# hT, the low weight parts and oT at other places in SBUF

## The chip, the cores and the metric

The kernel runs on 1 core of one Trainium2 chip. The metric is the device time of one execution in microseconds. The time before is the median of three runs, 1087.04 us (1086.99 to 1087.83).

## The reference

One decoder layer on a residual stream of 256 positions and 2048 channels, in float32. Cut to what matters here:

```python
h = rmsnorm(x, pre_mix_g)
proj = h @ w_in                               # 2048 x 4368
q_a, k_a, v_a, q_b, k_b, v_b, f_b = split(proj)
o_a = swa_sink_attention(q_a, k_a, v_a, sinks)     # 16 heads of 64, window 128, ALiBi, sinks
o_b = forgetting_attention(q_b, k_b, v_b, log_sigmoid(f_b + b_forget))   # 16 heads of 64
x = x + rmsnorm(concat(rmsnorm(o_a), rmsnorm(o_b)) @ w_out, post_mix_g)  # 2048 x 2048
h = rmsnorm(x, pre_ffn_g)
u = causal_dwconv(h @ w_up, conv_w, conv_b)        # 2048 x 11264, width 3
gate, val = split(u)
x = x + rmsnorm((gelu(gate) * val) @ w_down, post_ffn_g)   # 5632 x 2048
```

## The kernel before

Every matrix product is made exact enough by splitting both float32 operands into a high part (rounded to float32r) and a low part (the rest), and by adding three products: high by high, high by low, low by high. All weights come from HBM once, in units of 128 partitions by up to 1024 floats, issued by SP into the tile raw (5 buffers). ScalarE copies a unit into its high part whi (L111), and VectorE subtracts to get the low part wlo (L114); each has 5 buffers. TensorE then uses them in one of two ways.

*hT moves, weights stay.* hT holds the transposed input of the projection, for each of 16 k-tiles 512 columns: 256 of the high part, then 256 of the low part. It is a tile of 128 x 16 x 512 floats. `proj_T` makes the product for 256 output channels: its `high(u)` (L256) takes 128 x 128 pieces of whi as the stationary operand and moves all 512 columns of hT; its `low(u)` (L263) takes pieces of wlo and moves only the 256 high columns. Four units of four k-tiles make one projection, in runs of several units, so that up to 32 matmuls of one kind follow each other. `unit_T` (L220 and L225) does the same in the first projections, `first_gate` (L878 and L874) in the first one of the MLP, half a k-tile's columns at a time. The up-projection (w_up) runs like this in two stretches, from 356.79 to 588.11 us and from 707.81 to 955.53 us.

*Weights move, activations stay.* `mm3` (L278) takes a 128 x 128 piece of an activation as stationary operand and moves whi, wlo and whi again past it. It is used with hT for v (384 or 272 columns), with oT for the output projection (512 columns; 256 in one place) and with G for the down-projection (512 columns, and 256 at the end). oT are 16 tiles of 128 x 512, one for each pair of heads, written by the attention; G are 22 tiles of 128 x 512 with the MLP's inner activations. Near the end four units of w_down lie in the tile rest, which takes over hT's place.

`w_parts` hands out the tiles for a unit's two parts. Its argument held is true where the weights stay (first way), and false where they move. The wlo tile is 128 floats wider than a unit; with held the low part begins LOW = 56 floats (224 bytes) into it, and without it at its start.

The tiles are laid out by pools, in the order in which they are asked for. Two unused tiles stand around hT, of 48 and 80 floats, together 512 bytes. In the built program these are the places along a partition, as bytes past a multiple of 512: hT and rest 192, the low parts of held weights 224, and 0 for the high parts, the low parts of weights that move, all oT and all G.

The order of the work on TensorE is the order in which the code is written (a manual schedule), and most of the other engines' order is set by a scheduler. TensorE loads the stationary operand of the next matmul while the present one runs (PEld in the profile).

Of the kernel before, what the change touches and what calls it, by code (L numbers as in the profile page):

```python
# [8 lines left out]
F32 = mybir.dt.float32  # L9
F32R = mybir.dt.float32r  # L10
# [7 lines left out]
P = 128  # L18
# [6 lines left out]
NEG = -1e30  # L25
FHALF = 22
HOLD = 6
LOW = 56
ROOM = 112


# [1 line left out]
def hybrid_layer(ctx: ExitStack, tc: tile.TileContext, x, pre_mix_g, w_in, b_forget, sinks,  # L33
# [9 lines left out]
    main = ctx.enter_context(tc.tile_pool(name="main", bufs=1))  # L43
# [25 lines left out]
    def w_load(src, a, c, pin=False):  # L69
# [3 lines left out]
            tc.keep_in_program_order(i)  # L73
        return raw, a, c

    def w_parts(n, keep=None, held=True):

        if keep and keep[0] is None:
            return keep[1]
        where, pre, nb = (keep[0], "h", keep[1]) if keep else (wp, "w", WB)  # L80
        hi = where.tile([P, UNIT], F32R, tag=pre + "hi", bufs=nb, name="whi")
        if where is not wp:
            lo = where.tile([P, UNIT], F32R, tag=pre + "lo", bufs=nb, name="wlo")
            return hi[:, :n], lo[:, :n]
        lo = where.tile([P, UNIT + 128], F32R, tag=pre + "lo", bufs=nb, name="wlo")
        return hi[:, :n], lo[:, LOW * held:LOW * held + n]

    def w_high(unit, keep=None, held=True):

        raw, a, c = unit  # L90
        n = a * c
        hi, lo = w_parts(n, keep, held)
        act.copy(hi, raw[:, :n])

        def low():
            dve.tensor_tensor(lo, raw[:, :n], hi.bitcast(F32), op=ALU.subtract)

        return [x.rearrange("p (a c) -> p a c", a=a) for x in (hi, lo)], low

    def w_split(unit, pin=False, keep=None, begun=None, between=None,  # L100
                held=True):

        raw, a, c = unit
        n = a * c
        hi, lo = begun or w_parts(n, keep, held)
        for i in range(2 if between else 1):
            cs = slice(i * 512, i * 512 + 512) if between else slice(0, n)
            if i:
                between()
            if not between or i:  # L110
                i1 = act.copy(hi[:, cs], raw[:, cs])  # L111
                if pin:
                    tc.keep_in_program_order(i1)
            i2 = dve.tensor_tensor(lo[:, cs], raw[:, cs], hi[:, cs].bitcast(F32), op=ALU.subtract)  # L114
            if pin:
                tc.keep_in_program_order(i2)
        return [x.rearrange("p (a c) -> p a c", a=a) for x in (hi, lo)]

    def w_unit(src, a, c, keep=None):
        return w_split(w_load(src, a, c), keep=keep, held=False)  # L120

    def w_rows(w, k0, a, c0, c):
        return w[k0 * P:(k0 + a) * P, c0:c0 + c].rearrange("(a p) c -> p a c", p=P)
# [56 lines left out]
        pool.tensor_tensor(r, v, mhalf, op=ALU.pow)  # L180
        return r

    main.tile([P, 48], F32, tag="before_hT", name="before_hT")
    hT = main.tile([P, KT, 512], F32R, tag="hT", name="hT")
    main.tile([P, 80], F32, tag="behind_hT", name="behind_hT")
    def to_T(srcs, t0, n, g0, pin=False):

        for part in range(2):
            for kt, tb in srcs:
                hi = hT[:, kt, t0:t0 + n]  # L190
                gk = gcol[:, g0 + kt:g0 + kt + 1]
                if part == 0:
                    i = act.activation(hi, tb, AF.Copy, scale=gk)
                else:
                    i = dve.scalar_tensor_tensor(hT[:, kt, 256 + t0:256 + t0 + n], tb, gk,
                                                 hi.bitcast(F32), op0=ALU.mult, op1=ALU.subtract)
                if pin:
                    tc.keep_in_program_order(i)
# [83 lines left out]
        dve.tensor_tensor(lo, src, hi.bitcast(F32), op=ALU.subtract)  # L282

    with tc.tile_pool(name="mixp", bufs=1) as mp:
        oT = [mp.tile([P, 512], F32R, tag="oT", bufs=16, name=f"oT{j}")[:, 0:512] for j in range(16)]
        sqs = mp.tile([P, 2, S], F32, tag="sqs", name="sqs")

        att = tc.tile_pool(name="att", bufs=1)
# [43 lines left out]


        begun = w_parts(UNIT)
        tc.keep_in_program_order(dve.tensor_copy(begun[0][:, 0:512], head[:, 0:512]))
        x_part(0, (0,), "acc")
# [258 lines left out]
        for p0, npair, cols in ((0, 3, 384), (3, 3, 384), (6, 2, 272)):  # L595
# [3 lines left out]
            for k0 in range(0, KT, per):  # L599
                na = min(per, KT - k0)  # L600
                hi, lo = w_unit(w_rows(w_in, k0, na, c0, cols), na, cols)
# [207 lines left out]
    with tc.tile_pool(name="ffn", bufs=1) as fp:  # L809
# [89 lines left out]
        for half in range(2):  # L899
# [43 lines left out]
            for n in range(3 + (half == 0)):  # L943
                b2 = [bank(), bank()]
                for u in range(FHALF // 2):
                    hi, lo = w_unit(w_rows(w_down, half * FHALF + u * 2, 2, n * 512, 512), 2, 512)
# [32 lines left out]
        held = []  # L979
        for u in range(FHALF // 2):  # L980
            hi, lo = w_unit(w_rows(w_down, FHALF + u * 2, 2, 1536, 512), 2, 512,
                            keep=(None, [rest[:, c:c + 2, :].rearrange("p a c -> p (a c)")
                                         for c in (4 * (u - LAST), 4 * (u - LAST) + 2)])
                            if LAST <= u < FHALF // 2 - 4 else None)
# [56 lines left out]
```

## Time and profile before

| | |
|---|---|
| median of 3 runs | 1087.04 us |
| profiled execution | 1086.65 us |
| its span, first to last instruction | 1084.9 us |
| mean granted TensorE clock | 0.997 |
| PE busy | 1073.4 us, 5986 matmuls |
| PEld busy | 926.5 us |
| DVE, ACT, POOL busy | 734.1, 613.6, 224.8 us |
| read from HBM | 199.58 MB, 186 GB/s over the span |

How to read it: PE is TensorE's matmuls, PEld its weight loads, DVE the VectorE, ACT the ScalarE, POOL the GpSimd and SP the SyncE, which issues most DMAs. A row of a group gives the line, the engine, the operation, what is written and from what, the shape, the count, the busy time and the mean duration of one. A matmul's duration includes its way through the array, which the next one overlaps; so the distance between two starts is shorter than a duration, and the sum of these distances is what PE takes. Windows give the stretch, its length, each engine's busy time with a count, then the granted clock, the share of the DMA engines' time, and GB/s.

### The profile page before, as it was taken

How to read it: one execution, taken by the hardware profiler on the slowest of the kernel's cores; microseconds unless marked ns; L12 is line 12 of the kernel's file. 1: busy time of each engine (PE TensorE's matmuls, PEld its weight loads, DVE VectorE, ACT ScalarE, POOL GpSimd, SP SyncE). 2: the span in 40 equal slices, each digit the busy share in tenths (PEclk: the TensorE clock that was granted, in tenths of full speed). 3: DMA queues.
4: the chain of work that ended last, by engine and by line, in shares of the span. 5: the costliest groups of instructions: out<-in, count | busy, mean ns of one | idle time of the engine just before them, and what ended most of it. 6: DMA issues, size and time to landing. Idle time of an engine off the chain costs nothing.

```text
span 1084.9 us, 16263 instructions
## 1 busy us (share of the span) xinstructions
PE 1073.4 (99%) x5986; PEld 926.5 (85%) x5986; DVE 734.1 (68%) x1200; ACT 613.6 (57%) x1060; POOL 224.8 (21%) x252
## 2 busy tenths in 40 slices
PE   9999999999999999999999999999999999999996
PEld 7889988888889888888888888888888888888886
DVE  5978877776568867777677444457777777765563
ACT  7766766667547755555555444455555555544450
POOL 3343244331022212112121000012121211201111
PEclk9999999999999999999999999999999999999998
DMA  8645566554863765566555665656565555556652
GB/s 292 209 132 157 175 182 197 173 154 153 297 223 119 227 188 187 181 193 195 186 184 176 209 195 194 196 177 193 184 188 190 182 189 188 188 191 196 195 168 78
DMA packets 164970, 202.88 MB, mean 187 GB/s; under 512 B 6780, under 2 KB 130972, under 8 KB 164380
## 3 DMA queue, kind: packets, MB, share of 16 engines
q1 hardware_dynamic: 164176, 201.27, 58.5%
q8 instruction: 47, 0.77, 0.3%
q10 hardware_dynamic: 716, 0.58, 0.2%
q14 instruction: 31, 0.25, 0.1%
HBM read 199.58 MB, written 2.11 MB: 186 GB/s over the span
## 4 chain that ended last, share of the span: by engine, by line
PE 96%; DVE 1%; ACT 1%; DMA 1%; SPq 0%; issue 0%; POOL 0%; DVEq 0%; POOLq 0%; ACTq 0%
PE bank_acc L278 35%; PE bank_acc L256 23%; PE bank_att L256 14%; PE bank_acc L263 12%; PE bank_att L263 7%; PE bank_att L443 1%; PE bank_att L478 1%; PE bank_att L487 1%; PE bank_acc L220 1%; DMA x_in<-in_x_dram 1%; PE bank_att L220 1%; DVE wlo L114 0%; PE bank_att L489 0%; DVE hT L736 0%; PE bank_acc L225 0%; PE bank_acc L878 0%
## 5 line engine op out<-in xcount | busy, mean ns | idle before, releaser
L114 DVE TENSOR_TENSOR wlo<-raw,whi 128x1024 fp32r<-128x1024 f32 (+3 forms) x357 | 431.3, 1217 | 254.8 <-ACT whi L111 244.0
L111 ACT CAST whi<-raw 128x1024 fp32r<-128x1024 f32 (+3 forms) x356 | 363.6, 1035 | 284.5 <-issue 138.0
L256 PE MATMUL bank_acc<-hT,whi 128*128 128x512 f32 x1088 | 264.9, 395 | 0.0
L256 PEld LDWEIGHTS bank_acc<-hT,whi 128*128 128x128 f32 x1088 | 200.3, 188 | 45.0
L278 PE MATMUL bank_acc<-whi,G 128*128 128x512 f32 (+1 forms) x724 | 214.4, 378 | 0.0
L845 POOL TENSOR_TENSOR u<-u,rowf 128x256 f32<-128x256 f32 x88 | 98.0, 1136 | 504.6 <-DVE u L844 502.1
L278 PEld LDWEIGHTS bank_acc<-whi,G 128*128 128x128 f32 x724 | 133.7, 188 | 25.6
L256 PE MATMUL bank_att<-hT,whi 128*128 128x512 f32 x640 | 154.1, 395 | 0.0
L256 PEld LDWEIGHTS bank_att<-hT,whi 128*128 128x128 f32 x640 | 118.6, 188 | 27.4
L263 PE MATMUL bank_acc<-hT,wlo 128*128 128x256 f32 x1088 | 139.5, 282 | 0.0
L263 PEld LDWEIGHTS bank_acc<-hT,wlo 128*128 128x128 f32 x1088 | 135.6, 188 | 4.3
L278 PE MATMUL bank_acc<-wlo,G 128*128 128x512 f32 (+1 forms) x362 | 137.1, 379 | 0.0
L278 PE MATMUL bank_acc<-whi,oT 128*128 128x512 f32 (+1 forms) x272 | 82.4, 380 | 0.0
L263 PEld LDWEIGHTS bank_att<-hT,wlo 128*128 128x128 f32 x640 | 78.6, 188 | 1.8
L263 PE MATMUL bank_att<-hT,wlo 128*128 128x256 f32 x640 | 79.0, 281 | 0.0
L278 PEld LDWEIGHTS bank_acc<-wlo,G 128*128 128x128 f32 x362 | 68.1, 188 | 12.8
L278 PEld LDWEIGHTS bank_acc<-whi,oT 128*128 128x128 f32 x272 | 50.2, 188 | 9.2
L278 PE MATMUL bank_acc<-wlo,oT 128*128 128x512 f32 (+1 forms) x136 | 51.2, 377 | 0.0
L278 PE MATMUL bank_acc<-whi,hT 128*128 128x384 f32 (+1 forms) x192 | 47.6, 324 | 0.0
L847 ACT ACTIVATE yg<-u,cw 128x256 f32<-128x256 f32 x44 | 26.5, 603 | 27.2 <-POOL u L845 27.2
L847 ACT ACTIVATE yv<-u,cw 128x256 f32<-128x256 f32 x44 | 26.5, 603 | 26.1 <-POOL u L845 26.1
L461 ACT ACTIVATE p<-p,nm 128x256 f32<-128x256 f32 (+1 forms) x64 | 28.4, 445 | 20.9 <-DVE nm L449 20.9
(200 smaller groups left out, 1009.0 us busy)
## 6 DMA issues: line engine op xcount, KB each, us to landing
raw<-in_w_up_dram SPq DMA_DIRECT2D x176, 512.0 KB, 3.5
raw<-in_w_down_dram SPq DMA_DIRECT2D x88, 512.0 KB, 4.7
raw<-in_w_in_dram SPq DMA_DIRECT2D x51, 512.0 KB, 4.7
raw<-in_w_out_dram SPq DMA_DIRECT2D x32, 512.0 KB, 4.1
raw<-in_w_in_dram SPq DMA_DIRECT2D x16, 384.0 KB, 3.7
cb<-c_dram SPq DMA_DIRECT2D x8, 256.0 KB, 3.2
x_sb<-in_x_dram SPq DMA_DIRECT2D x2, 1024.0 KB
raw<-in_w_in_dram SPq DMA_DIRECT2D x5, 408.0 KB, 3.5
```

Source lines behind the costliest of these rows:

```text
L111: i1 = act.copy(hi[:, cs], raw[:, cs])
L114: i2 = dve.tensor_tensor(lo[:, cs], raw[:, cs], hi[:, cs].bitcast(F32), op=ALU.subtract)
L220: pe.matmul(b, hi[:, a, m * P:(m + 1) * P], hT[:, kt, 0:512], start=(kt == 0), stop=(kt == KT - 1))
L256: pe.matmul(b, hi[:, a, m * P:(m + 1) * P], hT[:, kt, 0:512], start=(kt == 0), stop=(last == (0, kt)))
L263: pe.matmul(b[:, 256:512], lo[:, a, m * P:(m + 1) * P], hT[:, u * 4 + a, 0:256], start=False, stop=(last == (1, u * 4 + a)))
L278: pe.matmul(b, a, r[:, cols], start=(first and i == 0), stop=(last and i == 2))
L443: pe.matmul(sb[e][:, cs], a[r, t * P:(t + 1) * P], b[r, 0:nk], start=(n == 0), stop=(n == 2))
L461: act.activation(p[:, e, cs], p[:, e, cs], AF.Exp, bias=nm[:, t, e:e + 1], scale=-1.0, accum_out=rs[:, t, e:e + 1])
L478: pe.transpose(pb[:, i * P:(i + 1) * P], p[:, e, c:c + P], ident)
L487: pe.matmul(ov, values(hl, 0), p[:, :, 0:256], start=(n == 0), stop=False)
L845: pool.tensor_tensor(u[:, 2:258], u[:, 2:258], rowf, op=ALU.mult)
L847: act.activation(y, u[:, 2:258], AF.Identity, bias=cw[:, 3, ch:ch + 1], scale=cw[:, 2, ch:ch + 1])
```

## The change

Three things change, all of them places in SBUF. The two unused tiles around hT go, so that hT (and rest) begins at a multiple of 512 bytes. The low part of held weights begins at one of 16 places in its tile, 0, 8, ... 120 floats (0 to 480 bytes), the next place with each unit. The oT tiles become 520 floats wide, and each block of 512 begins OFF[j] floats (0, 2 or 4) into its tile, so that the 16 blocks begin at 16 different places modulo 512 bytes (with the tiles' own starts at steps of 32 bytes, and 0, 8 or 16 bytes added). The high parts, the low parts of weights that move, and G stay at multiples of 512. Each engine has the same instructions in the same order.

```diff
-LOW = 56
+OFF = (2, 4, 4, 4, 0, 4, 0, 4, 0, 4, 4, 4, 0, 4, 4, 4)
 ...
+    place = [0]
+
     def w_parts(n, keep=None, held=True):
 ...
         lo = where.tile([P, UNIT + 128], F32R, tag=pre + "lo", bufs=nb, name="wlo")
-        return hi[:, :n], lo[:, LOW * held:LOW * held + n]
+        place[0] += held
+        at = place[0] % 16 * 8 * held
+        return hi[:, :n], lo[:, at:at + n]
 ...
-    main.tile([P, 48], F32, tag="before_hT", name="before_hT")
     hT = main.tile([P, KT, 512], F32R, tag="hT", name="hT")
-    main.tile([P, 80], F32, tag="behind_hT", name="behind_hT")
 ...
-        oT = [mp.tile([P, 512], F32R, tag="oT", bufs=16, name=f"oT{j}")[:, 0:512] for j in range(16)]
+        oT = [mp.tile([P, 520], F32R, tag="oT", bufs=16, name=f"oT{j}")[:, i:i + 512]
+              for j, i in enumerate(OFF)]
```

## The prediction

> **What bounds the kernel now.** I read the page first, then PE's waits, then the groups of instructions with shapes kept apart, then stretches of PE's timeline. The page says where the time lies.
>
> ```profile
> span 1084.9 us, 16263 instructions
> PE 1073.4 (99%) x5986; PEld 926.5 (85%) x5986; DVE 734.1 (68%) x1200; ACT 613.6 (57%) x1060; POOL 224.8 (21%) x252
> PE 96%; DVE 1%; ACT 1%; DMA 1%; SPq 0%; issue 0%; POOL 0%; DVEq 0%; POOLq 0%; ACTq 0%
> ```
>
> PE is busy 99% of the span and makes up 96% of the chain that ended last. A busy PE need not be a PE at its best, so the next question is whether it ever waits. Its waits, complete (who, for whom, us in total, times, longest):
>
> ```profile
> PE bank_acc L166 <- DVE junk L161: 1.3, 1, 1.3
> PE bank_acc L303 <- DMA x_in<-in_x_dram: 0.6, 1, 0.6
> PE bank_att L303 <- DMA x_in<-in_x_dram: 0.5, 1, 0.5
> PE bank_att L208 <- DVE diag L202: 0.3, 1, 0.3
> PE bank_att L478 <- DVE p L468: 0.3, 1, 0.3
> ```
>
> That is 3.0 us. The kernel's time is therefore the sum of the distances from one matmul's start to the next one's, which I call steps. A change that moves only addresses can act through the step alone. The groups that it touches, with their counts (busy, and the mean of one, which includes the drain and is longer than a step):
>
> ```profile
> L256 PE MATMUL bank_acc<-hT,whi 128*128 128x512 f32 x1088 | 264.9, 395 | 0.0
> L278 PE MATMUL bank_acc<-whi,G 128*128 128x512 f32 x652 | 202.7, 389 | 0.0
> L256 PE MATMUL bank_att<-hT,whi 128*128 128x512 f32 x640 | 154.1, 395 | 0.0
> L263 PE MATMUL bank_acc<-hT,wlo 128*128 128x256 f32 x1088 | 139.5, 282 | 0.0
> L263 PE MATMUL bank_att<-hT,wlo 128*128 128x256 f32 x640 | 79.0, 281 | 0.0
> L278 PE MATMUL bank_acc<-whi,oT 128*128 128x512 f32 x240 | 76.2, 392 | 0.0
> L278 PE MATMUL bank_acc<-wlo,oT 128*128 128x512 f32 x120 | 46.7, 389 | 0.0
> L278 PE MATMUL bank_acc<-whi,hT 128*128 128x384 f32 x128 | 34.8, 341 | 0.0
> L220 PE MATMUL bank_att<-hT,whi 128*128 128x512 f32 x32 | 9.1, 401 | 0.0
> L878 PE MATMUL bank_acc<-hT,whi 128*128 128x256 f32 x64 | 8.8, 282 | 0.0
> ```
>
> The same shape, 128x512, has a mean of 395 ns at L256 and 389 ns at L278 with G. The timeline tells what that is worth in steps (start, us, engine, line; xN matmuls in a row). A step is the next row's start less this one's, divided by N.
>
> ```profile
> 801.63 3.96 PE L263 MATMUL bank_acc<-hT,wlo 128*128 128x256 f32 x32
> 805.42 7.63 PE L256 MATMUL bank_acc<-hT,whi 128*128 128x512 f32 x32
> 812.89 3.96 PE L263 MATMUL bank_acc<-hT,wlo 128*128 128x256 f32 x32
> ```
>
> L256: (812.89 - 805.42)/32 = 233.4 ns. L263: (805.42 - 801.63)/32 = 118.4 ns. Now a whole stage of L278 with G, 512 columns each, as busy time of that line's matmuls:
>
> ```profile
> 588.12:707.81 119.69, 119.69 (x528) 1.00 0.62 195
> ```
>
> 119.69/528 = 226.7 ns at the full granted clock (the 1.00 after the count). So 512 columns take 233.4 ns at one line and 226.7 ns at another, 6.7 ns apart, with no wait in either.
>
> **What differs between the two.** In the built program before, hT begins 192 bytes past a multiple of 512, while whi, G and oT begin at a multiple. While one matmul streams its moving operand, the stationary operand of the next is loaded. I call "distance" the place of that next stationary operand less that of the moving one, modulo 512. L256 (hT moves, whi stays) has distance 0 - 192 = 320. L278 with G has 0. The trace holds a test of this within one line: near the end, some weights lie in the tile rest, which has hT's place, and they move against the same G.
>
> ```profile
> 1059.37 2.97 PE L278 MATMUL bank_acc<-rest,G 128*128 128x512 f32 x12
> 1062.17 0.39 PE L278 MATMUL bank_acc<-whi,G 128*128 128x512 f32 x1
> 1067.63 1.58 PE L278 MATMUL bank_acc<-rest,G 128*128 128x256 f32 x12
> 1069.05 0.28 PE L278 MATMUL bank_acc<-whi,G 128*128 128x256 f32 x1
> ...
> 1071.92 1.54 PE L278 MATMUL bank_acc<-rest,G 128*128 128x256 f32 x12
> 1073.30 0.28 PE L278 MATMUL bank_acc<-whi,G 128*128 128x256 f32 x1
> ```
>
> From rest at 512 columns: (1062.17 - 1059.37)/12 = 233.3 ns, which is L256's step. Twenty-four matmuls with whi follow, up to 1067.63: 5.46/24 = 227.5 ns. Line, shape and stationary tile are the same; the moving tile's place is not. At 256 columns it is the other way round: rest takes 1.42/12 = 118.3 and 1.38/12 = 115.0 ns, and the 24 matmuls with whi between 1069.05 and 1071.92 take 2.87/24 = 119.6 ns. So distance 0 is the better one for 512 columns and the worse one for 256.
>
> **The change part by part.** No instruction is added, removed or moved on any engine's queue or SP's; only addresses change. A shorter step needs its weights sooner, and the cover for that is seen in the stages that gain (busy of PE, PEld, DVE, ACT, POOL):
>
> ```profile
> 356.79:588.11 231.32, 231.32 (x1322) 201.82 (x1322) 167.88 (x249) 132.84 (x208) 46.68 (x42) 1.00 0.60 190
> 707.81:955.53 247.72, 247.72 (x1409) 215.11 (x1408) 174.12 (x254) 138.61 (x217) 46.90 (x42) 1.00 0.59 187
> ```
>
> DVE is busy 73% there at most, and the DMA share is 0.60. PE about 2% quicker does not reach either; if that cover were gone, the gain of these stages would go with it.
>
> *hT to a multiple of 512, high parts.* L256's distance becomes 0, which at 512 columns is 226.7 ns in 528 matmuls of another line. 1728 matmuls (1088 + 640) by 6.7 ns are -11.6 us. L220 has the same form (64 matmuls, 0.4 us), in the first 32 us, where the waits above lie; I take half, -0.2. Bounds: nothing, if distance is not the cause, and -12.0 in all.
>
> *Low parts at 16 places.* L263's distance is 224 - 192 = 32 now, and afterwards each of 0, 32, ... 480 in turn. Of the sixteen, 32 gives 118.4 ns, 0 gives 119.6, and 320 gives 115.0 to 118.3; the others are not known for this width. Bounds: all at 115.0 would be 1728 x -3.4 = -5.9 us, all at 119.6 would be +2.1. I take 118.0, near the row that has the same form, less a little for the places like 320: -0.7 us.
>
> *hT's other readers.* L878 (64 matmuls of 256 columns, whi at distance 320) goes to distance 0: at most 4.6 ns each, +0.3; I take +0.2. Where hT is stationary at L278 (192 matmuls of 384 columns, 96 of 272), the distance goes from 192 to 0:
>
> ```profile
> 75.11 0.34 PE L278 MATMUL bank_acc<-wlo,hT 128*128 128x384 f32 x1
> ...
> 79.27 0.34 PE L278 MATMUL bank_acc<-wlo,hT 128*128 128x384 f32 x1
> ```
>
> There are 24 matmuls between the two: 4.16/24 = 173.3 ns. The straight line between 119.6 ns (256) and 226.7 ns (512) gives 173.2 for 384 columns at distance 0, so I cost it at nothing, within 0.4 us for the narrow ones. The 12 wide matmuls from rest gain 0.1 and the 24 narrow ones lose as much.
>
> *oT's blocks at 16 distances.* They sit at 0 now:
>
> ```profile
> 288.89 0.39 PE L278 MATMUL bank_acc<-wlo,oT 128*128 128x512 f32 x1
> ...
> 318.13 0.39 PE L278 MATMUL bank_acc<-wlo,oT 128*128 128x512 f32 x1
> ```
>
> 129 matmuls in 29.24 us are 226.7 ns, the best step that the trace has for 512 columns, so there is more to lose than to gain. Bounds: 0, and 6.7 ns by 360 matmuls = +2.4 us. I take the middle, +1.2, less 0.1 for the 48 of 256 columns, which stand at the worse end.
>
> Sum: -11.6 - 0.2 - 0.7 + 0.2 + 1.1 = -11.2 us. The profiled execution took 1086.65 us (span 1084.9 and 1.75 around it), 0.39 below the median of the runs, 1087.04. Forecast: 1086.65 - 11.2 = 1075.5 us.
>
> **The rivals.** *Places do not matter* (the change does nothing): the 6.7 ns would come from something else in which L256 and L278 differ, and the time stays 1086.7 us. Against it stands the rest row, 233.3 against 227.5 ns within one line. [...]
>
> *Only the moving operand's place counts, not the distance.* The rest rows would read the same. L256 then gains in full, oT's places do nothing, and L263, which moves hT from a multiple of 512, goes to 119.6 ns: -11.8 + 2.1 + 0.2 = -9.5, so 1077.2 us. For it: hT stationary at 192 costs L278 nothing against the straight line. Against it: L263 (118.4) differs from the later rest row (115.0) with the moving operand at the same place and width.
>
> *The low parts eat the gain* (slower): at 256 columns PE loads 128 columns of weights for each short matmul, and thirteen of the sixteen places are unseen. The case decides for slower than no change once the average of the 16 exceeds 118.4 + 10.5/1.728 = 124.5 ns (10.5 us being the gain of all other terms). At 126.5 ns L263 would cost +14.0 us, and the time would be 1086.65 - 10.5 + 14.0 = 1090.2 us. Against it: no row of this width here has an average above 119.6.
>
> **How the numbers follow.** 0.2% (2.2 us) is about what a measurement of this kernel can tell from no change. My forecast has 0.74, the moving place alone 0.13, no effect 0.06, the low parts 0.04; 0.03 is left for a smaller gain that still counts. So faster 0.90, same 0.06, slower 0.04. Bounds of the forecast: 1086.65 - 12.0 - 5.9 = 1068.8 and 1086.65 - 11.6 + 2.1 + 2.4 + 0.7 = 1080.3. Both ends want all unknowns on one side; I give 1070 to 1080, which takes in the second rival.
>
> **What would show it.** In the trace afterwards, a row of 32 matmuls at L256 takes 7.25 us instead of 7.47, and L256's mean falls from 395 to about 389 ns. Rows of L263 differ from unit to unit, between 115 and 120 ns a step, about 118 in the mean. L278 with oT rises from 226.7 to some 230 ns, L278 with G stays. PE's waits stay near 3 us and its count is unchanged. The prediction is wrong if L256 stays at 233 ns, if L263 averages over 122 ns, or if PE begins to wait for wlo.

## The result, and the profile after

The changed kernel takes 1080.74 us (median of four runs, 1080.23 to 1081.30) against 1087.42 us before (four runs, 1086.99 to 1087.83): a ratio of 0.9939, 95% interval 0.9921 to 0.9956. It is 6.7 us faster where 11.2 were forecast, and 0.74 us above the range's end. The profiled execution took 1080.67 us, 6.0 less than the one before. The page after, first lines:

```profile
span 1079.0 us, 16263 instructions
PE 1066.5 (99%) x5986; PEld 928.1 (86%) x5986; DVE 735.4 (68%) x1200; ACT 613.2 (57%) x1060; POOL 225.7 (21%) x252
```

The span is 5.9 us shorter, and PE is busy 6.9 us less with the same 5986 matmuls. The largest waits of PE after:

```profile
PE bank_acc L170 <- DVE junk L165: 1.3, 1, 1.3
PE bank_att L222 <- ACT whi L115: 0.9, 1, 0.9
PE bank_acc L306 <- DMA x_in<-in_x_dram: 0.5, 1, 0.5
```

With four smaller ones they are 3.9 us, 0.9 more than before: the one for the first high part, at the start, is the largest of those that are new. So 6.9 less and 0.9 more make up the span, and the question is again the step. The groups of PE's matmuls after, by line, shape, count, busy us and mean ns (L256, L263, L278 and L878 before are L258, L265, L280 and L881 now):

```profile
L258 PE MATMUL bank_acc<-hT,whi 128*128 128x512 f32 x1088 | 259.4, 391 | 0.0
L280 PE MATMUL bank_acc<-whi,G 128*128 128x512 f32 x652 | 202.7, 389 | 0.0
L258 PE MATMUL bank_att<-hT,whi 128*128 128x512 f32 x640 | 150.5, 390 | 0.0
L265 PE MATMUL bank_acc<-hT,wlo 128*128 128x256 f32 x1088 | 139.5, 282 | 0.0
L265 PE MATMUL bank_att<-hT,wlo 128*128 128x256 f32 x640 | 79.0, 281 | 0.0
L280 PE MATMUL bank_acc<-whi,oT 128*128 128x512 f32 x240 | 77.2, 396 | 0.0
L280 PE MATMUL bank_acc<-wlo,oT 128*128 128x512 f32 x120 | 47.2, 394 | 0.0
L881 PE MATMUL bank_acc<-hT,whi 128*128 128x256 f32 x64 | 9.1, 287 | 0.0
```

Against the rows before, the high parts go from 264.9 + 154.1 to 259.4 + 150.5, which is -9.1 us; the low parts read the same to a tenth; oT costs 1.0 + 0.5 = +1.5; L881 +0.3; G nothing. These make -7.3, the other groups +0.4.

Now the timeline, in the stretch that the prediction used:

```profile
798.26 3.97 PE L265 MATMUL bank_acc<-hT,wlo 128*128 128x256 f32 x32
802.06 7.45 PE L258 MATMUL bank_acc<-hT,whi 128*128 128x512 f32 x32
809.35 3.93 PE L265 MATMUL bank_acc<-hT,wlo 128*128 128x256 f32 x32
813.12 3.80 PE L258 MATMUL bank_acc<-hT,whi 128*128 128x512 f32 x16
816.75 3.80 PE L258 MATMUL bank_att<-hT,whi 128*128 128x512 f32 x16
```

Thirty-two high matmuls take 7.29 us from start to start, 227.8 ns each, where 233.4 were taken before and 226.7 forecast. The low ones take 118.8 and 117.8 ns.

**The step inside a run.** I matched the starts of single matmuls in the trace to the addresses in the built program, and averaged the high matmuls over their 73 runs by their place in the run (interruptions at the ends of runs included, ns):

| place in the run | first | 2nd | 3rd | 4th | 5th | 6th | 7th | 8th on | last |
|---|---|---|---|---|---|---|---|---|---|
| before | 244.6 | 234.3 | 232.3 | 234.3 | 232.3 | 234.4 | 232.2 | 233.3 | 239.9 |
| after | 245.6 | 233.4 | 228.7 | 230.1 | 228.6 | 227.4 | 227.6 | 226.7 | 246.6 |

The settled step is exactly the forecast one, but a run needs five to seven matmuls to get there, and its last matmul, behind which a low part is loaded at another distance, is slower than before (246.6 ns against 239.9). Theory: the step depends on the distance and on the matmuls that ran before, so the gain of 6.7 ns is had only inside long runs. Rivals: hT's own place counts, not the distance; the low parts' rotation, or oT, takes back what hT gains.

### The profile page after: what moved, and what is told of

The parts are those of the page before. It is cut to its first block, busy times and chain, and to the rows that moved or that the text cites. A ratio compares the mean times of both kernels' runs of the same rounds, so it can differ in the third digit from the quotient of the medians.

```text
span 1079.0 us, 16263 instructions
## 1 busy us (share of the span) xinstructions
PE 1066.5 (99%) x5986; PEld 928.1 (86%) x5986; DVE 735.4 (68%) x1200; ACT 613.2 (57%) x1060; POOL 225.7 (21%) x252
## 4 chain that ended last, share of the span: by engine, by line
PE 95%; DVE 2%; DMA 1%; POOL 1%; ACT 1%; issue 0%; SPq 0%; DVEq 0%; POOLq 0%; ACTq 0%
PE bank_acc L280 35%; PE bank_acc L258 21%; PE bank_att L258 13%; PE bank_acc L265 11%; PE bank_att L265 7%; PE bank_att L446 1%; PE bank_att L481 1%; PE bank_att L490 1%; DMA x_in<-in_x_dram 1%; PE bank_acc L222 1%; PE bank_att L222 1%; DVE wlo L118 0%; PE bank_att L492 0%; DVE hT L739 0%; PE bank_acc L227 0%
## 5 line engine op out<-in xcount | busy, mean ns | idle before, releaser
L258 PE MATMUL bank_acc<-hT,whi 128*128 128x512 f32 x1088 | 259.4, 391 | 0.0
L258 PEld LDWEIGHTS bank_acc<-hT,whi 128*128 128x128 f32 x1088 | 200.8, 188 | 39.5
L280 PE MATMUL bank_acc<-whi,G 128*128 128x512 f32 (+1 forms) x724 | 214.4, 379 | 0.0
L280 PEld LDWEIGHTS bank_acc<-whi,G 128*128 128x128 f32 x724 | 133.8, 188 | 25.5
L258 PE MATMUL bank_att<-hT,whi 128*128 128x512 f32 x640 | 150.5, 390 | 0.0
L265 PE MATMUL bank_acc<-hT,wlo 128*128 128x256 f32 x1088 | 139.5, 282 | 0.0
L258 PEld LDWEIGHTS bank_att<-hT,whi 128*128 128x128 f32 x640 | 118.9, 188 | 23.6
L265 PEld LDWEIGHTS bank_acc<-hT,wlo 128*128 128x128 f32 x1088 | 135.4, 188 | 4.1
L280 PE MATMUL bank_acc<-wlo,G 128*128 128x512 f32 (+1 forms) x362 | 137.1, 379 | 0.0
L280 PE MATMUL bank_acc<-whi,oT 128*128 128x512 f32 (+1 forms) x272 | 83.4, 383 | 0.0
L265 PEld LDWEIGHTS bank_att<-hT,wlo 128*128 128x128 f32 x640 | 78.5, 188 | 1.7
L280 PEld LDWEIGHTS bank_acc<-wlo,G 128*128 128x128 f32 x362 | 68.1, 188 | 12.7
L265 PE MATMUL bank_att<-hT,wlo 128*128 128x256 f32 x640 | 79.0, 281 | 0.0
L280 PEld LDWEIGHTS bank_acc<-whi,oT 128*128 128x128 f32 x272 | 50.2, 188 | 10.2
L280 PE MATMUL bank_acc<-wlo,oT 128*128 128x512 f32 (+1 forms) x136 | 51.7, 380 | 0.0
L280 PE MATMUL bank_acc<-whi,hT 128*128 128x384 f32 (+1 forms) x192 | 47.6, 324 | 0.0
```

Of the source, the lines that this page charges most:

```text
L258: pe.matmul(b, hi[:, a, m * P:(m + 1) * P], hT[:, kt, 0:512], start=(kt == 0), stop=(last == (0, kt)))
L265: pe.matmul(b[:, 256:512], lo[:, a, m * P:(m + 1) * P], hT[:, u * 4 + a, 0:256], start=False, stop=(last == (1, u * 4 + a)))
L280: pe.matmul(b, a, r[:, cols], start=(first and i == 0), stop=(last and i == 2))
```

## The experiments

**hT alone.** The two tiles around hT go and nothing else; low parts stay 224 bytes into their tile, which is distance 224 now, and oT stays at 0.

```diff
-    main.tile([P, 48], F32, tag="before_hT", name="before_hT")
     hT = main.tile([P, KT, 512], F32R, tag="hT", name="hT")
-    main.tile([P, 80], F32, tag="behind_hT", name="behind_hT")
```

> Only hT moves to a multiple of 512 bytes; low parts stay at 224 bytes, oT at 0. Distance theory (a step is set by the next stationary operand's place less the moving one's): the 1728 long matmuls with hT moving gain as much as in the changed kernel, 8.8 us; the low ones now stand at distance 224, where the changed kernel's units took 117.8 ns a step against 119.3 before, so another 2.6 us; sum with the first gate's +0.3: -11 us, ratio 0.990. Rival (only the moving operand's place counts): the low ones go to the step of other 256-column matmuls that move from a multiple of 512, 119.6, so -8 us, ratio 0.9925.

Measured: 1075.90 us, ratio 0.9898 (0.9882 to 0.9913), 11.1 us faster. One third of the change alone does more than the whole. Its groups, and a stretch of its timeline (hT moves at L254 and L261 here):

```profile
L254 PE MATMUL bank_acc<-hT,whi 128*128 128x512 f32 x1088 | 259.3, 391 | 0.0
L254 PE MATMUL bank_att<-hT,whi 128*128 128x512 f32 x640 | 150.6, 390 | 0.0
L261 PE MATMUL bank_acc<-hT,wlo 128*128 128x256 f32 x1088 | 137.8, 281 | 0.0
L261 PE MATMUL bank_att<-hT,wlo 128*128 128x256 f32 x640 | 77.9, 279 | 0.0
```

```profile
798.01 7.45 PE L254 MATMUL bank_acc<-hT,whi 128*128 128x512 f32 x32
805.30 3.90 PE L261 MATMUL bank_acc<-hT,wlo 128*128 128x256 f32 x32
809.03 3.82 PE L254 MATMUL bank_acc<-hT,whi 128*128 128x512 f32 x16
```

The high parts gain 9.1 us, as in the changed kernel. The low parts gain another 1.7 + 1.1 = 2.8 us without being moved in their tiles: distance 224 takes 3.73/32 = 116.6 ns where 32 took 118.4. The rival's 119.6 ns does not appear. The rotation gives these 2.8 us up.

**hT and oT.** As the last, with oT's blocks at 16 places too.

```diff
-        oT = [mp.tile([P, 512], F32R, tag="oT", bufs=16, name=f"oT{j}")[:, 0:512] for j in range(16)]
+        oT = [mp.tile([P, 520], F32R, tag="oT", bufs=16, name=f"oT{j}")[:, i:i + 512]
+              for j, i in enumerate(OFF)]
```

> hT at a multiple of 512 and oT's blocks at 16 distances; low parts stay at 224 bytes. Distance theory: as with hT alone, and +1.4 us for oT (360 matmuls of 512 columns from 227 to about 231.5 ns): -9.6 us, ratio 0.991. Rival (moving place only): oT is stationary, so no difference to hT alone, and its steps stay at 227 ns.

Measured: 1077.97 us, ratio 0.9916 (0.9902 to 0.9929), 2.1 us behind hT alone, whose runs were made on the same chip beside it. Its groups with oT (L277) are those of the changed kernel:

```profile
L277 PE MATMUL bank_acc<-whi,oT 128*128 128x512 f32 x240 | 77.2, 396 | 0.0
L277 PE MATMUL bank_acc<-wlo,oT 128*128 128x512 f32 x120 | 47.2, 394 | 0.0
```

The rival that gives oT no part is out. Against hT alone, where they read 76.3 and 46.8 us, the trace shows 1.3 us of the 2.1. In the changed kernel the step comes from the first and the last row of a stretch, 57 groups of three matmuls apart:

```profile
284.11 0.40 PE L280 MATMUL bank_acc<-wlo,oT 128*128 128x512 f32 x1
...
323.69 0.40 PE L280 MATMUL bank_acc<-wlo,oT 128*128 128x512 f32 x1
```

39.58/171 = 231.5 ns, against 226.7 with all blocks at distance 0.

**The low parts alone.** The rotation without the rest; hT stays at 192 and oT at 0.

```diff
-        return hi[:, :n], lo[:, LOW * held:LOW * held + n]
+        place[0] += held
+        at = place[0] % 16 * 8 * held
+        return hi[:, :n], lo[:, at:at + n]
```

> Only the low parts rotate through the 16 places; hT stays at 192, oT at 0. Distance theory: the same set of distances as in the changed kernel, so the low matmuls average 119 ns and differ from unit to unit between 114 and 120; time unchanged within 1 us, ratio 1.000. Rival (moving place only): also 1.000, but all units alike at 118.5 ns in the middle of a run.

Measured: 1087.15 us, ratio 1.0002 (0.9994 to 1.0011). Its groups L267 (low) and L260 (high):

```profile
L267 PE MATMUL bank_acc<-hT,wlo 128*128 128x256 f32 x1088 | 139.5, 282 | 0.0
L260 PE MATMUL bank_acc<-hT,whi 128*128 128x512 f32 x1088 | 265.0, 397 | 0.0
```

The rotation by itself is worth nothing: 139.5 us as before it, while single units average from 113.3 to 120.2 ns a step (without their first and last). That is not the rival's "all alike". The average of its places is no better than distance 32.

**hT at 0, low parts at 64.** In the changed kernel, units at distance 64 showed the shortest low steps, 116.2 ns over all their starts. Here all have it.

```diff
-LOW = 56
+LOW = 16
```
(and the two tiles around hT are left out.)

> hT at a multiple of 512, all held low parts at 64 bytes, oT at 0. Distance theory: the long matmuls gain 8.8 us as in the changed kernel; low ones stand at distance 64 throughout, where the changed kernel's units took 116.2 ns against 119.3 before: -5.4 us; with +0.3 for the first gate -13.9 us, ratio 0.987. Rival (moving place only): low ones at 119.6, -8 us, ratio 0.9925.

Measured: 1076.95 us, ratio 0.9909 (0.9896 to 0.9923), a miss for both. Its low step (L261):

```profile
805.48 3.93 PE L261 MATMUL bank_acc<-hT,wlo 128*128 128x256 f32 x32
809.25 3.81 PE L254 MATMUL bank_acc<-hT,whi 128*128 128x512 f32 x16
```

3.77/32 = 117.8 ns, and single steps go on at 117 to 119 ns. A unit at 64 behind one at 32, as the changed kernel has it, steps otherwise (113.3 ns) than a unit at 64 behind one at 64. So the distance alone does not set the step; what ran before it counts. This trace shows the same without any change of place. The first row of L261 here follows attention's work, the second the high matmuls of its own projection, and 64 is the distance in both:

```profile
58.12 1.08 PE L261 MATMUL bank_acc<-hT,wlo 128*128 128x256 f32 x8
59.03 3.82 PE L254 MATMUL bank_acc<-hT,whi 128*128 128x512 f32 x16
62.69 2.05 PE L261 MATMUL bank_acc<-hT,wlo 128*128 128x256 f32 x16
64.58 0.81 PE L476 MATMUL bank_att<-ident,p 128*128 128x128 f32 x6
```

The first takes 0.91/8 = 114 ns a step and settles at 113 to 114; the second takes 1.89/16 = 118 and stays at 117 to 119. So this distance has two settled steps, 113.3 and 117.7 ns.

**Both shifted.** This separates the distance from the moving operand's own place. hT stays at 192 bytes, and held high parts begin 192 bytes into a longer tile, so their distance is 0; low parts begin at 0, distance 320.

```diff
-LOW = 56
+LOW = 48
...
-        lo = where.tile([P, UNIT + 128], F32R, tag=pre + "lo", bufs=nb, name="wlo")
-        return hi[:, :n], lo[:, LOW * held:LOW * held + n]
+        hi = where.tile([P, UNIT + 128], F32R, tag=pre + "hi", bufs=nb, name="whi")
+        lo = where.tile([P, UNIT], F32R, tag=pre + "lo", bufs=nb, name="wlo")
+        return hi[:, LOW * held:LOW * held + n], lo[:, :n]
```

> hT back at 192 bytes, and the high parts of held weights moved to 192 as well (distance 0); held low parts at 0 (distance 320, which is 64 modulo 256); oT at 0. Distance theory: long matmuls settle at 226.7 ns and gain as much as with hT at a multiple of 512 (about 9 us), low ones settle at 117.7 as at distance 64; 1077 us, ratio 0.991. Rival (only the moving operand's place counts, hT moves from 192): long ones stay at 233.4 and low ones at 118.4; 1087 us, ratio 1.000.

Measured: 1077.28 us against 1087.28, ratio 0.9909 (0.9895 to 0.9922), that of the last experiment. Its timeline:

```profile
799.97 7.44 PE L257 MATMUL bank_acc<-hT,whi 128*128 128x512 f32 x32
807.24 3.93 PE L264 MATMUL bank_acc<-hT,wlo 128*128 128x256 f32 x32
811.01 3.81 PE L257 MATMUL bank_acc<-hT,whi 128*128 128x512 f32 x16
```

7.27/32 = 227.2 ns with hT at its old place: the rival that only the moving operand's place counts would keep 233.4 and is out. The low parts take 117.8 ns at distance 320, what they took at 64, which is 320 less 256.

**More, shorter runs.** If runs need several matmuls to settle, cutting them to one unit (8 matmuls) must cost most of the gain. The same edit is made to the kernel before and to hT alone:

```diff
-    LONG = ((0, 1), (0, 1, 2, 3), (2, 3))
+    LONG = ((0,), (0,), (1,), (1,), (2,), (2,), (3,), (3,))
```

The kernel before with it:

> The kernel before with each long run of the MLP's up-projection cut into runs of one unit (8 long matmuls, then 8 low ones). By the steps at the beginning and end of runs (11 + 7 ns for the long, 17 + 11 for the low), some 131 more pairs of runs cost 6 us: 1093 us, ratio 1.0055. A rival for which run length plays no part: 1.000.

Measured: 1086.57 us, ratio 0.9994 (0.9985 to 1.0003). A miss: more runs cost the kernel before nothing. What the first and last matmuls of the table above take beyond a step is then no fixed price of a run; I had priced it from averages that hold the interruptions by attention's work.

hT alone with it:

> hT at a multiple of 512 (low parts at 224, oT at 0) with the same runs of one unit. Settling theory (a long matmul reaches 226.7 ns only after some six in a row, and the last before a low one costs more): long ones average 234.1 ns against 235.5 in the short-run kernel before, so they keep 2 of the 6.7 us that the MLP's 1376 had, low ones some 2 us; in all about 5.5 us less than the short-run kernel before, 1087.5 us. Rival (each matmul gains by its distance alone): 11 us less, as with long runs, 1082 us.

Measured: 1080.65 us, ratio 0.9940 (0.9926 to 0.9954), so 5.9 us below the kernel with the same runs, where long runs gave 11.1. The difference is the 5.5 of the settling theory and not the rival's 11; the time itself is nearer to the rival's 1082 than to 1087.5, which was built on the missed 1093. The two timelines, before with short runs first, then hT alone with them:

```profile
796.85 2.03 PE L256 MATMUL bank_acc<-hT,whi 128*128 128x512 f32 x8
798.72 1.11 PE L263 MATMUL bank_acc<-hT,wlo 128*128 128x256 f32 x8
799.67 2.03 PE L256 MATMUL bank_acc<-hT,whi 128*128 128x512 f32 x8
```

```profile
798.43 2.01 PE L254 MATMUL bank_acc<-hT,whi 128*128 128x512 f32 x8
800.28 1.10 PE L261 MATMUL bank_acc<-hT,wlo 128*128 128x256 f32 x8
801.21 2.01 PE L254 MATMUL bank_acc<-hT,whi 128*128 128x512 f32 x8
```

1.87/8 = 233.8 against 1.85/8 = 231.3 ns: a run of 8 gains 2.5 ns a matmul, a run of 32 gained 5.6. The eight steps, averaged over these runs of hT alone, are 232, 236, 228, 233, 231, 227, 227 and 235 ns: five until it settles, and the last one, behind which a low part is loaded. That is what settling and the end of a run cost, in a pair of kernels that differ in hT's place alone.

**A scan of the low parts' distance.** hT and oT at 0; the low parts' place changes only every 12 units, through steps of 16 bytes.

```diff
+SLOTS = (32, 64, 224, 16, 0, 48, 80, 96, 112, 128, 144, 160, 176, 192, 208, 240, 32, 224, 64, 0)
...
+        place[0] += held
+        at = SLOTS[place[0] // 12] // 4 * held
```

> hT at a multiple of 512, oT at 0, and the low parts' place held for 12 units (three projections) at a time, in steps of 16 bytes through 0 to 240. Distance theory with settling: each place has a repeating pattern of its own, with means between 114 and 122 ns; 32 gives 118.5, 64 117.7, 224 116.7 as when used throughout. Rival (the place in the turn, not the distance, makes the difference): all alike at 118. Open is whether a place below 116.7 exists.

Measured, one run of 1079.24 us; the step at 256 columns by distance, from single starts, to about half a nanosecond (0 and 16 from the fewest):

| bytes | 0 | 16 | 32 | 48 | 64 | 80 | 96 | 112 |
|---|---|---|---|---|---|---|---|---|
| ns | 119.6 | 118.6 | 118.2 | 118.3 | 117.4 | 118.7 | 117.3 | 120.0 |

| bytes | 128 | 144 | 160 | 176 | 192 | 208 | 224 | 240 |
|---|---|---|---|---|---|---|---|---|
| ns | 119.8 | 119.5 | 120.0 | 118.1 | 117.8 | 116.7 | 116.8 | 117.5 |

The eight at steps of 32 bytes, which the rotation goes through, average 118.4, the step of the kernel before. No constant place is below 116.7. Two rows show more (distance 208 throughout, then a run with 24 matmuls at 224 and the last 8 at 64):

```profile
786.18 3.89 PE L265 MATMUL bank_att<-hT,wlo 128*128 128x256 f32 x32
789.91 3.80 PE L258 MATMUL bank_att<-hT,whi 128*128 128x512 f32 x16
...
907.63 3.87 PE L265 MATMUL bank_att<-hT,wlo 128*128 128x256 f32 x32
911.34 7.44 PE L258 MATMUL bank_att<-hT,whi 128*128 128x512 f32 x32
```

3.73/32 = 116.6 ns for the one, 3.71/32 = 115.9 for the other, although 64 and 224 alone take 117.4 and 116.8: the last eight, at 64, settle at 113.3. Here a place reached from another one is better than either. It is no rule: 240, reached from 208 in the same trace, took 120.0 for its eight, where it takes 117.3 when it is kept.

**32, then 64.** So the order was used: in each run of low matmuls the first unit lies at 32 bytes and the others at 64, with hT and oT at 0.

```diff
+        begins = [us[0] for us in runs[1::2]]
...
             if u not in parts:
+                LOWAT[0] = 8 if u in begins else 16
                 parts[u] = w_split(w_load(w_rows(w, u * 4, 4, c0, 256), 4, 256))
+                LOWAT[0] = 56
```
(`w_parts` uses LOWAT[0] where it used LOW.)

> hT at a multiple of 512, oT at 0; in each run of low matmuls the first unit's low part stands at 32 bytes and those that follow at 64. In the changed kernel a unit at 64 that followed one at 32 took 113.3 ns a step, while with 64 throughout it took 117.6. Carry-over theory (a short matmul's step depends on the state that the ones before left as well as on the distance): the first unit 118.4, the rest of the run 113.3; over 32 that is 114.6 against 116.7 with 224 throughout, so some 3 us under hT alone, 1073 us, ratio 0.987. Rival (the distance alone sets the settled step): 117.8 throughout, 1 us over hT alone, 1077 us, ratio 0.991.

Measured: 1073.75 us against 1087.21, ratio 0.9877 (0.9862 to 0.9893): 13.5 us faster than before, and faster than the changed kernel, timed beside it, by 6.2. Its low groups and a run:

```profile
L264 PE MATMUL bank_acc<-hT,wlo 128*128 128x256 f32 x1088 | 136.3, 279 | 0.0
L264 PE MATMUL bank_att<-hT,wlo 128*128 128x256 f32 x640 | 76.6, 277 | 0.0
```

```profile
803.56 3.83 PE L264 MATMUL bank_acc<-hT,wlo 128*128 128x256 f32 x32
807.23 3.81 PE L257 MATMUL bank_acc<-hT,whi 128*128 128x512 f32 x16
```

3.67/32 = 114.7 ns a step over the run, and from the tenth matmul of a run on 113.3, with a distance that took 117.7 in such runs when it was never left. That is the carry-over, used. It need not be 32 that goes before: 224 did it in the scan, and attention's work did it before some of the runs with 64 throughout. Nor is 32 always enough: with the rotation alone and hT at 192, units at distance 64 that follow one at 32 as the last of a run average 118. Whether a first unit at 224, which takes less than one at 32, does better still was not tried.

**The changed kernel again**, beside the last one on the same chip.

> The changed kernel once more, beside the one above on the same chip. Both theories: 1080.7 us, ratio 0.994, and the same steps as in its first profile; a first 45 us that differs from the first profile's by up to 1 us would show that part as scatter of the start, not of the change.

Measured: 1079.97 us, ratio 0.9935 (0.9922 to 0.9947), span 1078.0. Its wait for the first high part:

```profile
PE bank_att L222 <- ACT whi L115: 0.3, 1, 0.3
```

0.3 instead of 0.9 us. By 45 us into the span this execution is 0.8 us ahead of the first profile of the same kernel. Over the profiles of the kernels here, the first 45 us vary from 0.6 us less to 1.1 more than before. So that part of the first profile is scatter.

## Why the prediction was right or wrong

The direction held, and so did one half of the mechanism: the gain is one of steps, and the settled step at distance 0 is 226.7 ns. The other half, that a matmul's step follows from its own distance alone, failed, and the size with it. By terms, forecast and measured in the profiled execution:

| term | forecast | measured | where it went |
|---|---|---|---|
| L256, high parts | -11.6 | -8.8 to -9.1 | settling of each run |
| L263, low parts | -0.7 | 0 to +0.2 | average of the places near 118.4, ends of runs +0.5 |
| oT | +1.1 | +1.5 | about 231.5 ns, not 230 |
| L878 | +0.2 | +0.3 | as bounded |
| PE's waits | 0 | +0.9 | mostly scatter at the start |

*The step that failed* is "1728 matmuls by 6.7 ns". The 226.7 ns were taken from 528 matmuls of one long stage, the 233.4 from one run of 32, and the difference was given to every matmul of 73 runs. By the table of places, the first of a run loses (6.7 + 1.0) x 73 = 0.6 us of it, the second to seventh 15.6 ns x 73 = 1.1 us, the last (6.7 + 6.7) x 73 = 1.0 us: 2.7 us, and -11.6 + 2.7 = -8.9. In its place the runs show a settled step that a run reaches only after five to seven matmuls, and a slower last one; the term measured -8.8 to -9.1. The pair of kernels with short runs shows these two apart from all else. Two signs stood in the prediction's own rows. The 24 matmuls with whi behind those from rest take 227.5 ns and not 226.7; their single steps are 226, 235, 229, 232, 231, 227, and 226 or 227 from there on, which is the settling. And the two rows from rest at 256 columns have the same line, shape and distance, 320, but take 118.3 and 115.0 ns: single steps of the first are 117 to 119, those of the second 113 to 114 from the fourth on. The prediction took the two as the bounds of one value; they are the two settled steps of this distance.

*The low parts* were taken at 118.0 ns, "near the row that has the same form, less a little". The average stayed within the bounds of 115.0 and 119.6, but the value was a guess toward the gain; the scan gives 118.4 for the average, so constant places would give 0. In the changed kernel itself some places differ from the scan's (64 takes 113.3 there, 96 takes 120.0), and the average inside units, 118.1, comes out near it all the same. By single starts the boundaries between runs add 0.5 us and the steps inside give back 0.3.

*oT* went to a little above the middle of its bounds. By distance, from single starts at 512 columns in the changed kernel: 226.7 ns at 0 and 227 at 240, 229.5 to 230.5 at 8, 256, 432 and 496, 231.5 at 128 and 384, about 233.3 at 80, 304, 320 and 368. None is below the 226.7 of distance 0. But a block meets only three or six matmuls in a row, so most of these are no settled steps.

*hT as the stationary operand* and G cost nothing, as forecast: whi past hT at 384 columns reads 34.8 us before and 34.9 after, whi past G at 512 columns 202.7 in both. (The moving pieces of 272 columns begin 0, 64 or 128 bytes past a multiple of 512, so for two of the three the distance does not go from 192 to 0, as the prediction has it, but to 448 or 384; their groups, 12.9 us with whi and 9.2 with wlo, read the same to 0.1 us.) *The waits* cost 0.9 us more in the first profile, mostly by the one for the first high part, which the second profile of the same kernel has at a third of that size. A small one is new with the change: PE waits 0.3 us for POOL's sqs in both profiles of the changed kernel, and not in the one before.

The sum of the errors, 2.7 + 0.9 + 0.4 + 0.1 + 0.9 (the waits) = 5.0 us, is what separates -11.2 from the -5.9 of the span within 0.3. The range took L256 at -11.6 even at its slow end; of that term's bounds, nothing and -12.0, it used only the one.

The rivals: *places do not matter* is refuted by hT alone, 11.1 us from two tiles that nobody reads: one shape takes 226.7 or 233.3 ns, by the two operands' distance. *Only the moving operand's place* gave 1077.2 us, nearer to the result than my own forecast, and is refuted all the same: with hT at its old place and the weights shifted the step was 227.2 ns, and the output projection, where whi moves from a multiple of 512 before and after and only the stationary oT shifts, became slower (231.5 ns a step against 226.7). *The low parts eat the gain* (slower than before) did not come, but it looked at the right place: against hT alone, the rotation gives up 2.8 us.

What would show it: a row of 32 at L256 takes 7.29 us, between the 7.25 forecast and 7.47; its mean is 391 and 390, not 389; L263's units differ as said; oT's step is 231.5 instead of some 230; G stays.

*Open:* what happens inside. The runs show that the step changes with the distance (at 512 columns 226.7 ns at 0 and 233.4 at 320) and with the matmuls before (at 256 columns and distance 64, 113.3 or 117.7 ns); by what means, no run here shows. Why distance 64 has two settled steps, and what decides between them, is not explained.

## What to carry to other kernels

When PE is busy 99% and waits for nothing, compare steps of one shape between lines; if they differ, compare where the stationary and the moving operand begin. Here distance 0 was the best for 512 columns (226.7 ns, against 233.4 at 320). At 256 columns search for the order of places: 32 and then 64 gave 114.7 ns over a run of 32, against 118.4 before, while going through all places in turn was worth nothing (ratio 1.0002). Before multiplying a difference of steps by a count, look at it by place in the run: here, at 512 columns and distance 0, the settled step of 226.7 ns belonged only to what came after the first five to seven matmuls of a run.

## What the runs showed of the hardware that was not expected

- At 256 columns, distances that are 256 bytes apart gave the same step, so counting them modulo 512, as the prediction did, told apart places that read alike. In the changed kernel the low steps inside units at distances 0 and 256 are 118.5 and 118.5 ns, at 64 and 320 113.3 and 113.3, at 96 and 352 120.0 and 120.0, and the other five pairs agree as well, to 0.1; 320 with both shifted equals 64 (117.8). At 512 columns these runs do not settle whether the same holds: oT's block at 256 averages 229.5, but it is met for six matmuls at most, and in one such stretch they take 235, 229, 232, 231, 227 and 226 ns, as a run at distance 0 begins.
- The step at 256 columns depends on what ran before as well: at one distance, 64, it settles at 117.7 or at 113.3 ns.
- Reaching the settled step takes five to seven matmuls at 512 columns (distance 0), and two at 256 where a unit at 64 follows the first at 32 (115.8 and 114.2 ns, then 113.3).
